# A weight quarter added by VectorE instead of an accumulating DMA, and weight buffers from a list instead of a ring

## The chip, the cores and the metric

One core of a Trainium2 chip runs the whole kernel as one program. The metric is the device time of one execution in microseconds, lower is better.

The core has five engines with queues of their own, each worked through in order: TensorE (PE: matmuls, and their weight loads, PEld), VectorE (DVE), ScalarE (ACT), GpSimd (POOL) and SyncE (SP). DMAs are issued from SP's queue or POOL's queue and run beside the engines. An engine that waits for a semaphore holds up all that stands behind in its queue.

## The reference

Two layers of a streaming encoder in float32, 512 tokens, width 1024. Cut to what matters:

```python
for i in range(2):
    h = h + 0.5 * swiglu_ffn(rms_norm(h, ffn1_norm[i]), ffn1_w_in[i], ffn1_w_out[i])
    u = rms_norm(h, mix_norm[i])
    ...                                    # SSD heads and latent attention on u @ w_in_mix[i]
    h = h + concat([y_ssd, y_mla]) @ w_out_mix[i]
    h = h + 0.5 * swiglu_ffn(rms_norm(h, ffn2_norm[i]), ffn2_w_in[i], ffn2_w_out[i])
    gate = sigmoid(rms_norm(h, ple_norm[i]) @ w_ple_gate[i])
    h = h + gate * (p[i] @ w_ple_proj[i])
return rms_norm(h, final_norm)

def swiglu_ffn(x, w_in, w_out):            # w_in: 1024 x 5632, w_out: 2816 x 1024
    g, u = jnp.split(x @ w_in, 2, axis=-1)
    return (jax.nn.silu(g) * u) @ w_out
```

So there are four FFN stages, two in each layer, and the change is in their first product, `x @ w_in`.

## The kernel before

**Precision.** Every float32 operand is split into two parts, `hi` (ScalarE's cast to the matmul's type, L300 for weights) and `lo` (VectorE's difference, L301). A product is three matmuls: hi by hi, hi by lo, lo by hi.

**The fast product.** In the FFN stages `x @ w_in` is computed for most columns in groups of 512, by a two-by-two scheme with seven block products in place of eight. There are nine groups in each stage (`NG`), 36 in all. For group `n` the weights are cut into four quarters of 512 x 256 by half of the inner dimension (`kh`) and half of the columns (`c`). Products 1, 2 and 3 (their numbers are names in the scheme) use the quarters (0,0), (1,0) and (1,1) as they are. Products 5, 6, 4 and 7 use sums of quarters, which are built in place, in a chain: 5 is 1's block plus quarter (0,1); 6 is 5's plus (1,1); 4 is 6's plus (1,0); 7 is 3's block plus (0,1). Each addition can start only when the block has been split for the product before it in the chain.

Before the groups come four whole blocks (`whole("g", f)`, f0 to f3), with which the norm's statistics overlap. The order of the products is written out: `FIRST_ORDER` for the first group (1, 5, 2, 3, 6) and `ORDER` for the others, where the 7 and the 4 of the group before are mixed in (1, 2, 7 of the group before, 5, 4 of the group before, 3, 6). The last group's 7 and 4 come after it, with whole blocks between them and behind.

**The units and their queue.** All weight blocks of the kernel stand in one list, `units`, in the order in which they are used. A unit either has a raw block of its own to load (`raws`, loaded by SP with L283, 512 KB in the FFN) or takes over the block of an earlier unit with something added. The function `weights(key)` hands out the next unit; before that it loads up to `LOOK_DMA` = 3 raw blocks beyond what the next units need and splits `LOOK_SPLIT` = 2 units ahead. `split_one` casts, subtracts and, where the block goes on in a chain (`more`), adds: by VectorE (L311) from another raw block, or by a DMA that accumulates from HBM into the block (L314, issued from POOL's queue).

In the kernel before, 5's and 7's additions are accumulating DMAs, 6's is a VectorE addition of 3's raw block before that is split, and 4's is a VectorE addition of 2's raw block, which was kept for it. A group has three loads, two accumulating DMAs and two VectorE additions.

**The raw buffers.** There are `NRAW` = 6 of 4 KB a partition, in one pool with one tag; a new tile takes a slot of this ring when the tile that held it is no longer used. The same ring gives temporaries: squares for the norms (L477 to L479), the FFN's output step (L762 to L765), and the attention's probabilities (L1260).

**Order on the engines.** The framework takes the program, and orders each engine's instructions by a simulated timeline; semaphores are set by it from the reads and writes of tiles.

Of the kernel before, what the change touches and what calls it, by code (L numbers as in the profile page):

```python
# [9 lines left out]
F32 = mybir.dt.float32  # L10
# [7 lines left out]
P = 128  # L18
# [77 lines left out]
def kernel(ctx: ExitStack, tc: tile.TileContext, a: dict, out: bass.AP):  # L96
# [5 lines left out]
    banks = _Slots(  # L102
        ctx.enter_context(tc.tile_pool(name="banks", bufs=1, space=bass.MemoryType.PSUM)), 8, "b"
    )
    p_raw = ctx.enter_context(tc.tile_pool(name="p_raw", bufs=NRAW))
    p_hi = ctx.enter_context(tc.tile_pool(name="p_hi", bufs=NW))
    p_lo = ctx.enter_context(tc.tile_pool(name="p_lo", bufs=NW))
    small = ctx.enter_context(tc.tile_pool(name="small", bufs=2))
# [6 lines left out]

    uid = [0]

    def tmp():

        uid[0] += 1  # L120
        return p_raw.tile([P, 1024], F32, tag="raw", name=f"tmp{uid[0]}")[:, :T]

    def sm(tag, shape, dt=F32, bufs=None):
        uid[0] += 1
# [12 lines left out]
    def raw(nk, cols, *loads):  # L137
        raws.append((nk, cols, loads))
        return len(raws) - 1
# [7 lines left out]
    def plan_ffn(i, nm, w_in, w_out):  # L147
        wq = w_in.rearrange("(k two p) f -> two p k f", two=2, p=P)

        def quarter(n, kh, c):  # L150
            x, q = GROUPS[n]
            c0 = q * 4 * P + (x == "u") * FF + c * 2 * P
            return [(slice(0, 2 * P), wq[kh, :, :, c0:c0 + 2 * P])]

        at = {}

        def quarter_unit(n, p):
            key = (i, nm, n, p)
            first = {1: (0, 0), 2: (1, 0), 3: (1, 1)}
            if p in first:  # L160
                unit(key, 4, 256, *quarter(n, *first[p]))
                at[n, p] = (len(units) - 1, units[-1][3])
            else:


                before = {5: 1, 6: 5, 4: 6, 7: 3}[p]
                add = {6: 3, 4: 2}.get(p)
                units.append((key, 4, 256, None, (at[n, before][0], quarter(n, 0, 1) if add is None else at[n, add][1])))
                at[n, p] = (len(units) - 1, None)

        def whole(x, f):
            unit((i, nm, x, f), KD, P, (None, kview(w_in, 0, KD, (x == "u") * FF + f * P, P)))

        for f in range(4):
            whole("g", f)
        for n in range(NG):
            for p, back in ORDER if n else FIRST_ORDER:
                quarter_unit(n - back, p)
        quarter_unit(NG - 1, 7)
        whole("g", LAST)  # L180
        quarter_unit(NG - 1, 4)
        whole("g", LAST + 1)
        whole("u", LAST)
        whole("u", LAST + 1)
        for m in range(KD):
            for k0 in range(0, KF, 8):
                nk = min(8, KF - k0)
                unit((i, nm, "o", m, k0), nk, P, (None, kview(w_out, k0, nk, m * P, P)))
# [70 lines left out]
    loaded, split, held = [], [], {}  # L259
    later = deque()  # L260
    more = {u[4][0]: j for j, u in enumerate(units) if u[4] is not None}

    def place_in(t, nk, cols, loads, start):
        v = t[:, :nk * cols].rearrange("p (k f) -> p k f", k=nk)
# [13 lines left out]
    def load_one():  # L278
        for _ in range(4 if len(loaded) > 2 else 0):
            if later:  # L280
                later.popleft()()
        t = p_raw.tile([P, 1024], F32, tag="raw", name=f"raw{len(loaded)}")
        place_in(t, *raws[len(loaded)], lambda dst, src: nc.sync.dma_start(out=dst, in_=src))  # L283
        loaded.append(t)

# [3 lines left out]
    def split_one():  # L289
        j = len(split)  # L290
        _, nk, cols, r, _ = units[j]
        if r is not None:
            while len(loaded) <= r:
                load_one()
            held[j] = loaded[r]
        x = held.pop(j)
        n = nk * cols
        hi = p_hi.tile([P, 1024], F32R, tag="hi", name=f"hi{j}")
        lo = p_lo.tile([P, 1024], F32R, tag="lo", name=f"lo{j}")
        A.copy(hi[:, :n], x[:, :n])  # L300
        V.tensor_tensor(lo[:, :n], x[:, :n], hi[:, :n].bitcast(F32), op=ALU.subtract)  # L301
        split.append((hi[:, :n].rearrange("p (k f) -> p k f", k=nk),
                      lo[:, :n].rearrange("p (k f) -> p k f", k=nk)))
        if j in more:

            held[more[j]] = x
            _, nk, cols, _, (_, add) = units[more[j]]
            if isinstance(add, int):
                while len(loaded) <= add:
                    load_one()  # L310
                V.tensor_tensor(x[:, :n], x[:, :n], loaded[add][:, :n], op=ALU.add)  # L311
            else:
                place_in(x, nk, cols, add,
                         lambda dst, src: G.dma_start(out=dst, in_=src, accum_op=ALU.add))  # L314

    taken = [0]

# [4 lines left out]
    def weights(key):  # L322
        j = taken[0]
        assert units[j][0] == key, (units[j][0], key)
        taken[0] += 1
        while len(loaded) < min(last_raw[min(j + LOOK_SPLIT, len(units) - 1)] + 1 + LOOK_DMA, len(raws)):
            load_one()
        while len(split) < min(j + 1 + LOOK_SPLIT, len(units)):
            split_one()
        got, split[j] = split[j], None  # L330
        return got
# [103 lines left out]
    class Norm:  # L435
# [36 lines left out]
        def add_square(self, src):  # L472
            if self.acc is None:
                self.acc = S()
                A.activation(self.acc.ap, src, AF.Square)
            else:
                sq = tmp()  # L477
                A.activation(sq, src, AF.Square)
                V.tensor_tensor(self.acc.ap, self.acc.ap, sq, op=ALU.add)  # L479

        @property
        def ops(self):
# [93 lines left out]
    def ffn(i, nm, norm, nxt, start=lambda: None, tables=lambda: None, between=lambda: None):  # L576
# [169 lines left out]
        for m in range(KD):  # L746
            b = B()
            for k0 in range(0, KF, 8):
                w = weights((i, nm, "o", m, k0))
                nk = w[0].shape[1]  # L750
                if m == 0:
                    while len(H) < min(k0 + nk, LAST):
                        split_pair(len(H) // 2)
                    if k0 + nk == KF:
                        split_last()
                acc_wx(b.ap, w, {f: (p.ap, q.ap) for f, (p, q) in H.items()}, k0, k0 == 0, k0 + 8 >= KF)
                if m == KD - 1:
                    for f in range(k0, k0 + nk):
                        slots.put(*H[f])
            if m == KD - 1:  # L760
                between()
            t = tmp()  # L762
            V.scalar_tensor_tensor(out=t, in0=b.ap, scalar=0.5, in1=norm.rb.ap, op0=ALU.mult, op1=ALU.mult)
            banks.put(b)
            V.tensor_tensor(h[m].ap, h[m].ap, t, op=ALU.add)  # L765
            nxt.add(h[m].ap)
        slots.put(norm.rb)

# [71 lines left out]
    def mixer(i, norm, nxt):  # L840
# [403 lines left out]
        def scores(hd, qb):  # L1244
            n = (qb + 1) * P
            qs = slice(qb * P, (qb + 1) * P)
            b = B()
            ql, kl = qh[hd], kh[hd]
            kr = st["kr"]
            mm(b[:, :n], lhsT=ql[0][:, qs], rhs=kl[0][:, :n], start=True, stop=False)  # L1250
            mm(b[:, :n], lhsT=ql[0][:, qs], rhs=kl[1][:, :n], start=False, stop=False)
            mm(b[:, :n], lhsT=ql[1][:, qs], rhs=kl[0][:, :n], start=False, stop=False)
            mm(b[:, :n], lhsT=qrow[hd][:, qs], rhs=kr[0][:, :n], start=False, stop=False)
            mm(b[:, :n], lhsT=qrow[hd][:, qs], rhs=kr[1][:, :n], start=False, stop=False)
            mm(b[:, n - P:n], lhsT=mk_l, rhs=mk_r, start=False, stop=True)
            m = sm("a_m", [P, 1], bufs=4)
            V.tensor_reduce(out=m, in_=b[:, :n], axis=AX.X, op=ALU.max)
            nb = sm("a_nb", [P, 1], bufs=4)
            V.tensor_tensor(nb, m, st["nsq"][:, qb:qb + 1], op=ALU.mult)
            pr = tmp()  # L1260
            rs = sm("a_rs", [P, 1], bufs=4)
            A.activation(pr[:, :n], b[:, :n], AF.Exp, bias=nb, scale=st["sq"][:, qb:qb + 1], accum_out=rs)
            banks.put(b)
            ri = sm("a_ri", [P, 1], bufs=4)
            V.reciprocal(ri, rs)
            V.tensor_scalar(pr[:, :n], pr[:, :n], ri, None, op0=ALU.mult)
            return pr
# [5 lines left out]
        def flip(hd, qb, pr, pt):  # L1273
            b = B()
            ks = order[qb]
            for n, kb in enumerate(ks):
                tr(b[:, n * P:(n + 1) * P], pr[:, kb * P:(kb + 1) * P], ident)  # L1277
            n = 0
            while n < len(ks):
                kb = ks[n]  # L1280
                w = 2 if (kb == 1 and qb == 3) else 1
                buf, c0 = place[kb]
                c0 += (qb - kb) * P
                src = b[:, n * P:(n + w) * P]
                halves(src, pt[0][buf][:, c0:c0 + w * P], pt[1][buf][:, c0:c0 + w * P])
                n += w
            banks.put(b)
# [284 lines left out]
```

## Time and profile before

| | |
|---|---|
| median of 3 runs | 2336.83 us (2334.89 to 2343.46) |
| the profiled execution's own time | 2346.55 us |
| its span, from the first to the last instruction | 2344.9 us |
| TensorE busy | 2295.8 us (98%) |
| VectorE busy | 1552.6 us (66%) |
| ScalarE busy | 1093.3 us (47%) |
| GpSimd busy | 215.5 us (9%) |
| moved by DMA | 229.01 MB, mean 98 GB/s |

How to read the profile: busy shares are means over stages. The groups of instructions give line, engine, operation, written and read tile, shape, count, then busy time, mean of one in ns, and the idle time of the engine just before them with what ended it (`<-`). In a timeline the first two numbers are start and duration in us, and a bracket gives the idle time before and its releaser. Rows of windows give the stretch, its length, then busy time and number of instructions for each engine, the granted TensorE clock as a share of full speed, the busy share of the 16 DMA engines, and GB/s. `raw` is a tile of the weight ring, `hi` and `lo` its two parts, `b` a PSUM bank, `s` a slot of working memory. L591 to L593 are the matmuls of the seven products, L418 to L420 those of whole blocks. The four FFN stages begin at about 0, 760, 1180 and 1920 us.

### The profile page before, as it was taken

Reading aid. Unit: us, or ns where it says so; the run is one execution under the profiler, and the core shown is the slowest. Engines: PE = TensorE matmul, PEld = TensorE weight load, DVE = VectorE, ACT = ScalarE, POOL = GpSimd, SP = SyncE. Lnnn points to the kernel's source line nnn. Section 1 sums busy time; section 2 is a strip of 40 time slices with the busy share of each in tenths; the row PEclk is TensorE's granted clock in tenths of the full one; section 3 lists DMA queues with packets and bytes.
Section 4 is the critical chain, followed back from the end, with each engine's and each line's share of the span. In section 5 each row is a group of like instructions: output and inputs, shape, how many; then the busy total and the mean of one; then the engine's idle time right before and its main releaser. Section 6 shows DMA issues by size and latency. Waiting matters only on the chain.

```text
span 2344.9 us, 34036 instructions
## 1 busy us (share of the span) xinstructions
PE 2295.8 (98%) x13542; PEld 2021.8 (86%) x13542; DVE 1552.6 (66%) x2456; ACT 1093.3 (47%) x1780; POOL 215.5 (9%) x208
## 2 busy tenths in 40 slices
PE   8999999999999899999999999999999999999998
PEld 6999888878888899888899988888788878998887
DVE  7878445678676777734777684466876776776345
ACT  6555324445455545522544452254544554454224
POOL 1110001132000111000011100012310001110000
PEclk9999999999999999999999999999999999999999
DMA  6555334311221465533345553342112225664332
GB/s 148 133 129 133 97 96 113 86 42 50 61 74 54 108 136 127 136 86 88 103 109 128 126 128 90 91 111 81 34 50 76 72 65 116 135 135 111 92 86 72
DMA packets 341420, 229.01 MB, mean 98 GB/s; under 512 B 20015, under 2 KB 335629, under 8 KB 341261
## 3 DMA queue, kind: packets, MB, share of 16 engines
q1 hardware_dynamic: 303244, 189.08, 27.5%
q0 software_dynamic: 38016, 37.75, 10.8%
q8 instruction: 106, 1.74, 0.3%
q14 instruction: 54, 0.43, 0.1%
HBM read 224.71 MB, written 2.10 MB: 97 GB/s over the span
## 4 chain that ended last, share of the span: by engine, by line
PE 81%; issue 10%; DVE 4%; DMA 2%; ACT 2%; POOL 1%; SPq 1%; POOLq 0%; ACTq 0%; DVEq 0%
PE b L418 15%; PE b L420 15%; PE b L419 15%; PE b L591 7%; PE b L593 7%; PE b L592 7%; DMA raw<-in_ffn_w_in_dram 2%; PE b L427 2%; PE b L426 2%; PE b L428 2%; DVE lo L301 1%; PE b L1112 1%; ACT hi L300 1%; PE b L1277 1%; DVE s L432 1%
## 5 line engine op out<-in xcount | busy, mean ns | idle before, releaser
L301 DVE TENSOR_TENSOR lo<-raw,hi 128x1024 fp32r<-128x1024 f32 (+3 forms) x536 | 612.4, 1143 | 469.6 <-ACT hi L300 469.0
L300 ACT CAST hi<-raw 128x1024 fp32r<-128x1024 f32 (+3 forms) x536 | 523.8, 979 | 855.6 <-PE b L419 411.5
L418 PE MATMUL b<-s,hi 128*128 128x512 f32 (+1 forms) x1754 | 693.5, 397 | 7.8 <-ACT hi L300 7.8
L420 PE MATMUL b<-s,lo 128*128 128x512 f32 (+1 forms) x1754 | 685.8, 392 | 6.5 <-DVE lo L301 6.5
L419 PE MATMUL b<-s,hi 128*128 128x512 f32 (+1 forms) x1754 | 683.8, 390 | 0.0
L591 PE MATMUL b<-s,hi 128*128 128x256 f32 x2016 | 574.4, 286 | 18.0 <-ACT hi L300 9.9
L592 PE MATMUL b<-s,hi 128*128 128x256 f32 x2016 | 572.0, 284 | 0.0
L593 PE MATMUL b<-s,lo 128*128 128x256 f32 x2016 | 567.9, 285 | 1.7 <-DVE lo L301 1.7
L591 PEld LDWEIGHTS b<-s,hi 128*128 128x128 f32 x2016 | 390.1, 193 | 23.5 <-ACT hi L300 11.7
L418 PEld LDWEIGHTS b<-s,hi 128*128 128x128 f32 x1754 | 330.6, 188 | 77.4 <-ACT hi L300 10.7
L420 PEld LDWEIGHTS b<-s,lo 128*128 128x128 f32 x1754 | 329.9, 188 | 77.6 <-DVE lo L301 8.8
L592 PEld LDWEIGHTS b<-s,hi 128*128 128x128 f32 x2016 | 390.2, 194 | 0.2
L593 PEld LDWEIGHTS b<-s,lo 128*128 128x128 f32 x2016 | 387.2, 193 | 2.6 <-DVE lo L301 2.5
L419 PEld LDWEIGHTS b<-s,hi 128*128 128x128 f32 x1754 | 330.5, 188 | 68.0 <-issue 2.9
L314 POOL DMA_DIRECT2D raw<-in_ffn_w_in_dram x72 | 92.8, 1289 | 850.5 <-DVE lo L301 819.2
L431 ACT CAST s<-b 128x128 fp32r<-128x128 f32 (+2 forms) x196 | 67.2, 361 | 99.8 <-DVE s L432 38.7
L431 ACT CAST s<-s 128x256 fp32r<-128x256 f32 (+1 forms) x248 | 94.2, 423 | 36.8 <-DVE s L611 13.2
L432 DVE TENSOR_TENSOR s<-s,s 128x256 fp32r<-128x256 f32 (+1 forms) x248 | 100.2, 442 | 9.8 <-PE b L593 7.4
L432 DVE TENSOR_TENSOR s<-b,s 128x128 fp32r<-128x128 f32 (+2 forms) x196 | 75.9, 401 | 30.2 <-ACT s L431 29.1
L503 POOL TENSOR_TENSOR nr<-nv,half 128x4 f32<-128x4 f32 (+1 forms) x14 | 20.2, 1439 | 813.1 <-DVE nv L495 812.3
L311 DVE TENSOR_TENSOR raw<-raw,raw 128x1024 f32<-128x1024 f32 x72 | 88.0, 1222 | 1.7
L426 PE MATMUL b<-hi,s 128*128 128x512 f32 (+1 forms) x208 | 78.5, 377 | 0.0
(245 smaller groups left out, 2247.7 us busy)
## 6 DMA issues: line engine op xcount, KB each, us to landing
raw<-in_ffn_w_in_dram SPq DMA_DIRECT2D x140, 512.0 KB
raw<-in_ffn_w_in_dram POOLq DMA_DIRECT2D x72, 512.0 KB, 5.9
raw<-in_ffn_w_out_dram SPq DMA_DIRECT2D x64, 512.0 KB
raw<-in_w_in_mix_dram SPq DMA_DIRECT2D x50, 512.0 KB
raw<-in_w_out_mix_dram SPq DMA_DIRECT2D x32, 512.0 KB
raw<-in_ffn_w_out_dram SPq DMA_DIRECT2D x32, 384.0 KB
raw<-in_w_ple_gate_dram SPq DMA_DIRECT2D x16, 512.0 KB
raw<-in_w_q_b_dram SPq DMA_DIRECT2D x16, 192.0 KB
```

The costliest lines, as they stand in the source:

```text
L300: A.copy(hi[:, :n], x[:, :n])
L301: V.tensor_tensor(lo[:, :n], x[:, :n], hi[:, :n].bitcast(F32), op=ALU.subtract)
L314: lambda dst, src: G.dma_start(out=dst, in_=src, accum_op=ALU.add))
L418: mm(b, lhsT=hi[:, kk, cs], rhs=xh, start=st, stop=False)
L419: mm(b, lhsT=hi[:, kk, cs], rhs=xl, start=False, stop=False)
L420: mm(b, lhsT=lo[:, kk, cs], rhs=xh, start=False, stop=en)
L426: mm(b, lhsT=xh[:, cs], rhs=hi[:, kk], start=first, stop=False)
L431: A.copy(hi, src)
L432: V.tensor_tensor(lo, src, hi.bitcast(F32), op=ALU.subtract)
L591: mm(o, lhsT=hi[:, k, cs], rhs=xh, start=first and f == k == 0, stop=False, **more)
L592: mm(o, lhsT=hi[:, k, cs], rhs=xl, start=False, stop=False, **more)
L593: mm(o, lhsT=lo[:, k, cs], rhs=xh, start=False, stop=f == 1 and k == 3, **more)
```

## The change

Quarter (0,1) gets a raw block of its own, loaded by SP right after product 1's block. Product 5's sum is a VectorE addition from it, behind the split of unit 1; the added block's buffer is then given back. Product 4's sum, until now a VectorE addition of 2's block, becomes an accumulating DMA of quarter (1,0) from HBM; 2's buffer is given back after its split. Products 6 and 7 are summed as before. A group has now four loads, two accumulating DMAs and two VectorE additions.

The six raw buffers have tags of their own and are given out from a list, the one that has been free longest first. They are given back in the program's text where the last use stands, for temporaries too. Loading ahead stops when only one buffer is free.

```diff
-    p_raw = ctx.enter_context(tc.tile_pool(name="p_raw", bufs=NRAW))
+    rawbufs = _Slots(ctx.enter_context(tc.tile_pool(name="p_raw", bufs=1)), NRAW, "raw")
...
-    def tmp():
-        uid[0] += 1
-        return p_raw.tile([P, 1024], F32, tag="raw", name=f"tmp{uid[0]}")[:, :T]
+    def W():
+        return rawbufs.get(F32, (P, 1024))
...
             if p in first:
                 unit(key, 4, 256, *quarter(n, *first[p]))
-                at[n, p] = (len(units) - 1, units[-1][3])
+                if p == 1:
+                    at[n, 0] = raw(4, 256, *quarter(n, 0, 1))
             else:
-                before = {5: 1, 6: 5, 4: 6, 7: 3}[p]
-                add = {6: 3, 4: 2}.get(p)
-                units.append((key, 4, 256, None, (at[n, before][0], quarter(n, 0, 1) if add is None else at[n, add][1])))
-                at[n, p] = (len(units) - 1, None)
+                before = at[n, {5: 1, 6: 5, 4: 6, 7: 3}[p]]
+                if p == 5:
+                    add = at[n, 0]
+                elif p == 6:
+                    add = units[at[n, 3]][3]
+                else:
+                    add = quarter(n, *{4: (1, 0), 7: (0, 1)}[p])
+                units.append((key, 4, 256, None, (before, add)))
+            at[n, p] = len(units) - 1
...
+    own = {u[3] for u in units}
...
-        t = p_raw.tile([P, 1024], F32, tag="raw", name=f"raw{len(loaded)}")
+        t = W()
         place_in(t, *raws[len(loaded)], lambda dst, src: nc.sync.dma_start(out=dst, in_=src))
...
-                V.tensor_tensor(x[:, :n], x[:, :n], loaded[add][:, :n], op=ALU.add)
+                y = loaded[add]
+                V.tensor_tensor(x[:, :n], x[:, :n], y[:, :n], op=ALU.add)
+                if add not in own:
+                    rawbufs.put(y)
             else:
                 place_in(x, nk, cols, add,
                          lambda dst, src: G.dma_start(out=dst, in_=src, accum_op=ALU.add))
+        else:
+            rawbufs.put(x)
...
-        while len(loaded) < min(last_raw[min(j + LOOK_SPLIT, len(units) - 1)] + 1 + LOOK_DMA, len(raws)):
+        while (len(loaded) < min(last_raw[min(j + LOOK_SPLIT, len(units) - 1)] + 1 + LOOK_DMA, len(raws))
+               and len(rawbufs.free) > 1):
             load_one()
```

The squares of the norms, the output step's temporary and the attention's probabilities take `W()` where they took `tmp()`, and each is followed by a `rawbufs.put` behind its last use.

More of the change, by code (lines that the diff above doesn't have):

```diff
@@ L476, in add_square @@
             else:
-                sq = tmp()
-                A.activation(sq, src, AF.Square)
-                V.tensor_tensor(self.acc.ap, self.acc.ap, sq, op=ALU.add)
+                sq = W()
+                A.activation(sq[:, :T], src, AF.Square)
+                V.tensor_tensor(self.acc.ap, self.acc.ap, sq[:, :T], op=ALU.add)
+                rawbufs.put(sq)
         @property
@@ L761, in ffn @@
                 between()
-            t = tmp()
-            V.scalar_tensor_tensor(out=t, in0=b.ap, scalar=0.5, in1=norm.rb.ap, op0=ALU.mult, op1=ALU.mult)
+            t = W()
+            V.scalar_tensor_tensor(out=t[:, :T], in0=b.ap, scalar=0.5, in1=norm.rb.ap, op0=ALU.mult, op1=ALU.mult)
             banks.put(b)
-            V.tensor_tensor(h[m].ap, h[m].ap, t, op=ALU.add)
+            V.tensor_tensor(h[m].ap, h[m].ap, t[:, :T], op=ALU.add)
+            rawbufs.put(t)
             nxt.add(h[m].ap)
@@ L1259, in scores @@
             V.tensor_tensor(nb, m, st["nsq"][:, qb:qb + 1], op=ALU.mult)
-            pr = tmp()
+            pr = W()
             rs = sm("a_rs", [P, 1], bufs=4)
@@ L1277, in flip @@
                 tr(b[:, n * P:(n + 1) * P], pr[:, kb * P:(kb + 1) * P], ident)
+            rawbufs.put(pr)
             n = 0
```

## The prediction

> **What bounds the kernel now.** I read the busy shares, the groups, the stage windows, the gaps of TensorE, and the queues of ScalarE and GpSimd around each gap.
>
> ```profile
> span 2344.9 us, 34036 instructions
> PE 2295.8 (98%) x13542; PEld 2021.8 (86%) x13542; DVE 1552.6 (66%) x2456; ACT 1093.3 (47%) x1780; POOL 215.5 (9%) x208
> ...
> L314 POOL DMA_DIRECT2D raw<-in_ffn_w_in_dram x72 | 92.8, 1289 | 850.5 <-DVE lo L301 819.2
> L311 DVE TENSOR_TENSOR raw<-raw,raw 128x1024 f32<-128x1024 f32 x72 | 88.0, 1222 | 1.7
> ```
>
> TensorE is the bound; no matmul is added or removed, so what can be won is its idle time (2344.9 - 2295.8 = 49 us) and time at a lowered clock. The windows show where that lies in the four FFN stages (columns: PE busy, weight loads, DVE, ACT, POOL, granted clock, DMA share, GB/s).
>
> ```profile
> core 0: us, PE busy (x) PEld busy (x) DVE busy (x) ACT busy (x) POOL busy (x), PEclk, DMA share, GB/s
> 40.00:60.00 20.00, 18.32 (x134) 17.73 (x133) 12.81 (x20) 10.66 (x14) 4.15 (x3) 0.91 0.58 130
> 780.00:800.00 20.00, 15.03 (x97) 14.11 (x96) 7.77 (x15) 6.75 (x9) 3.62 (x3) 0.83 0.45 88
> 800.00:820.00 20.00, 19.00 (x159) 18.82 (x158) 15.77 (x18) 11.17 (x15) 1.89 (x2) 1.00 0.49 114
> 820.00:960.00 140.00, 140.00 (x1169) 140.00 (x1168) 108.14 (x122) 72.11 (x96) 18.11 (x15) 1.00 0.60 132
> 1220.00:1340.00 120.00, 116.74 (x964) 115.69 (x964) 88.26 (x96) 58.30 (x74) 15.42 (x12) 1.00 0.57 126
> 1340.00:1360.00 20.00, 17.51 (x134) 17.34 (x133) 14.08 (x19) 8.41 (x13) 2.25 (x2) 0.91 0.49 113
> 1940.00:1960.00 20.00, 15.72 (x110) 15.22 (x109) 10.47 (x17) 10.15 (x14) 3.27 (x2) 0.83 0.37 61
> 1960.00:1980.00 20.00, 19.04 (x159) 18.87 (x158) 16.14 (x18) 8.83 (x11) 2.55 (x2) 1.00 0.55 122
> ```
>
> From 820 to 960 nothing is lost: a product of 24 matmuls takes 140 / 1169 x 24 = 2.87 us, a group of seven 20.1 us. The loss sits at the stage starts and along the third FFN stage. At the second stage's start:
>
> ```profile
> 779.02 1.33 POOL L314 DMA_DIRECT2D raw<-in_ffn_w_in_dram  x1 [110.95 <-DVE lo L301]
> ...
> 789.53 2.94 ACT L300 CAST hi<-raw 128x1024 fp32r<-128x1024 f32 x3 [11.50 <-DMA raw<-in_ffn_w_in_dram]
> ...
> 790.63 0.58 PE L591 MATMUL b<-s,hi 128*128 128x256 f32 x1 [4.50 <-ACT hi L300]
> ...
> 792.00:793.00 1.00, 1.00 (x5) 1.00 (x6) 1.00 (x2) 0.95 (x2) 1.00 (x1) 0.50 0.00 0
> ```
>
> In the first group product 5 comes right after product 1. Its weights are product 1's block with a quarter accumulated onto it by a DMA (L314), which starts only when unit 1 has been split. It needs 10.4 us; ScalarE, in order, stands 11.5 us at the cast of unit 5, with the casts of 2 and 3 behind it; TensorE stands 4.50 us, and the clock then falls to 0.50. The others are the same wait:
>
> ```profile
> 44.72 2.95 ACT L300 CAST hi<-raw 128x1024 fp32r<-128x1024 f32 x3 [6.40 <-DMA raw<-in_ffn_w_in_dram]
> ...
> 803.62 7.74 DMA raw<-in_ffn_w_in_dram
> 811.46 1.06 ACT hi L300
> ...
> 1218.20 1.05 ACT L300 CAST hi<-raw 128x1024 fp32r<-128x1024 f32 x1 [4.44 <-DMA raw<-in_ffn_w_in_dram]
> ...
> 1344.02 1.05 ACT L300 CAST hi<-raw 128x1024 fp32r<-128x1024 f32 x1 [4.65 <-DMA raw<-in_ffn_w_in_dram]
> ...
> 1945.67 2.94 ACT L300 CAST hi<-raw 128x1024 fp32r<-128x1024 f32 x3 [10.81 <-DMA raw<-in_ffn_w_in_dram]
> ...
> ACT hi L300 <- DMA raw<-in_ffn_w_in_dram: 82.8, 22, 11.5
> ```
>
> **The change part by part.**
>
> *Unit 5's sum goes from a DMA to VectorE.* The wait above goes away: behind the split of unit 1 stands one L311 add of 1.22 us instead of an accumulation of 7.7 to 10.4 us. The windows give what the waits cost. Idle: 1.68 + 4.97 + 1.00 + 3.26 + 2.49 + 4.28 + 0.96 = 18.6 us. Clock: 0.09 x 20 = 1.8 us in each of two windows; 0.17 x 20 = 3.4 us in each of the other two, of which some 0.8 falls on idle time counted already, so 2.6. Together 18.6 + 2 x 1.8 + 2 x 2.6 = 27.4 us. That is the most this part can give.
>
> The Trainium skill, "TensorE: Matmul & The Clock Gate", section "Why this matters for your kernels", has the clock drop only after TensorE gaps of some 3 us. By it the windows at 40 and 1340, with gaps of at most 1.68 and 2.49 us, would hold no clock loss and the gain would be 23.8 us. This trace disagrees (0.91 in both).
>
> What is late next at a stage start: the load of the added block. It stands in SP's queue directly behind unit 1's load, where unit 2's stood:
>
> ```profile
> 762.23 0.37 SPq L283 DMA_DIRECT2D raw<-in_ffn_w_in_dram  x1
> 769.03 0.37 SPq L283 DMA_DIRECT2D raw<-in_ffn_w_in_dram  x1
> 773.59 0.37 SPq L283 DMA_DIRECT2D raw<-in_ffn_w_in_dram  x1
> 776.18 3.88 SPq L283 DMA_DIRECT2D raw<-in_ffn_w_in_dram  x3
> ...
> 777.51 1.22 DVE L301 TENSOR_TENSOR lo<-raw,hi 128x1024 fp32r<-128x1024 f32 x1
> ```
>
> Counting the stage's loads (f0 to f3, 1, 2, 3), unit 1's is that of 762.23; the added block takes the place at 769.03, units 2 and 3 those of 773.59 and 776.18. Unit 1's split ends at 778.7, over 9 us after 769.03, so the add finds its data, unit 5 is cast by 781, and TensorE, which ran out at 786, has it in time. Units 2 and 3 come one load later but without the accumulation beside them. Residue 0, bounds 0 to 1 us a stage.
>
> *Unit 4's sum goes from VectorE to a DMA.* The adds stay 72 of 1.22 us: one moves from behind the split of 6 to behind that of 1, with three units between the adds as before; what is queued behind it on VectorE is the split of unit 2 and the combinations of products, which have a lookahead of two products (5.7 us). Zero; if that cover were gone, 36 x 1.22 = 44 us. The accumulations stay 72. Unit 4's starts after the split of 6 and is needed five units later (1, 2, 7, 5, 4), 14.3 us; unit 7's start and need stay as they are. On GpSimd nothing in a group waits behind them but each other. Their landing:
>
> ```profile
> DMA to landing us min/median/max: 5.6/5.9/10.4
> ...
> 213.50 1.28 POOL L314 DMA_DIRECT2D raw<-in_ffn_w_in_dram  x1 [13.05 <-DVE lo L301]
> ...
> 219.44 1.05 ACT L300 CAST hi<-raw 128x1024 fp32r<-128x1024 f32 x1 [1.11 <-DMA raw<-in_ffn_w_in_dram]
> ...
> 223.24 0.50 PE L418 MATMUL b<-s,hi 128*128 128x512 f32 x1 [0.85 <-ACT hi L300]
> ```
>
> Split (1.05 + 1.22) and even 10.4 us of landing fit into 14.3. Where it is tight is a stage's end: unit 7's cast already waits 1.11 us there, the next unit's cast is behind it and TensorE stands 0.85 us. Unit 4's accumulation now follows one product behind unit 7's and shares the engines with it. Bounds: 0 (the first lands in 5.9 us as now) to 10.4 - 5.9 = 4.5 us later, for each of four stages 0 to 18 us. I take 1 us each, near the lower end, since unit 7's starts first: 4 us.
>
> *36 loads of 512 KB more.* SP: 36 x 0.37 = 13 us of issue, hidden in its waiting; the DMA engines:
>
> ```profile
> q1 hardware_dynamic: 303244, 189.08, 27.5%
> ...
> SPq L283 <- DVE lo L301: 1226.5, 213, 22.2
> ```
>
> 0.275 x 2344.9 / 189.08 = 3.4 us per MB, so 1.8 us of 16 engines per load; in a group of 20.1 us the share goes from 0.60 to 0.69. Zero while the engines have room; 36 x 1.8 = 64 us if they had none.
>
> *A list instead of a ring.* I walked the list by hand for an FFN stage. In a group four buffers come free (the added block, unit 2's, 7's, 4's), each load takes the one freed an event before the last, so it can start six to seven units (17 to 20 us) before it is needed; in the ring unit 1's next block waits for unit 4's split, three units ahead (8.6 us). The free list never goes below one there. The squares and temporaries take the same list; at the first stage's start they rotate over three buffers. Bounds -2 to +3 us, taken 0.
>
> **Sum.** The profiled execution took 2346.55 us for its span of 2344.9 and is 9.7 us above the median. On its own time: 2346.55 - 27.4 + 4 = 2323.2. Against the median: if the third stage's chain of gaps (3.26 + 2.49 + 1.8 = 7.5 us), which the same code does not show in the other three stages, is most of the excess, 2336.83 - 19.9 + 4 = 2320.9; if none of it is, 2313.4. I take 2320, near the first, since that chain is nearly as long as the excess.
>
> **Rivals.**
> - *The wait moves to the stage ends.* The two accumulations, now one product apart among more loads, land late; the cast of unit 7 holds the next whole block up. For it: the 0.85 us gap there, and 10.4 us of landing while SP's loads ran. Against: unit 7's is issued first. Price: 4.5 us and 1.8 us of clock in each of two stages, 12.6: 2333; in all four, 2345. The Trainium skill, "DMA: Bandwidth & Descriptors", section "SWDGE vs HWDGE vs iDMA", has each DMA engine take turns between GpSimd's and SP's queues, which speaks for this. The 10.4 us beside three loads agrees with it.
> - *Slower: the add blocks VectorE.* In every group the add stands in order on the added block's load. If that comes later than 3.4 us (two products less 2.3 us of split) after unit 1's split, unit 2 is late and TensorE stands. At 4.5 us late, 1.1 us in 36 groups: 2320 + 40 = 2360. Against: 17 us of lead, and no cast waited for an SP load before.
> - *No gain.* TensorE meets another wait at the same places, such as unit 3's block for the add that makes unit 6: 2337. For it: VectorE runs 108 of 140 us there; against: the clean 140 us from 820.
>
> **How the numbers follow.** Forecast 0.62 (2311 to 2327), stage ends 0.22, blocking add 0.08, no gain 0.08. This measurement can tell some 0.5% (11.7 us) from nothing: faster means under 2325.1. Faster: the forecast less 0.04 above that bound, 0.58. Same: 0.04 + 0.18 of the stage ends + 0.08 = 0.30. Slower: 0.04 of the stage ends in full + 0.08 = 0.12. The range is 2310 to 2334, from the sum with no excess in the chain and the list's lower bound to the stage ends' first price; outside lie the blocking add, no gain and the tail of the stage ends.
>
> **What would show it.** Right: the casts' wait for DMA (82.8 us) falls under 20; the windows at the stage starts come to 20 us of TensorE at 1.00; L311 and L314 stay at 72; DMA bytes rise by 18.9 MB. Wrong: VectorE's add waiting on a load in many groups; TensorE gaps over 2 us at the stage ends; a chain of gaps that persists through a stage with unit 4's or 7's accumulation as its cause.

## The result, and the profile after

The changed kernel takes 2308.67 us (median of 5, 2306.83 to 2311.27) against 2336.83 us, 28.2 us less: ratio 0.9876, 95% interval 0.9857 to 0.9895. Forecast were 2320 us and a range that ended at 2310. The direction and the mechanism held; the gain was larger than forecast. The profiled execution took 2306.83 us, 39.7 us less than the one profiled before.

The page of the kernel after (L306 and L307 are now the weight split, L318 VectorE's addition, L323 the accumulating DMA, L604 the products' first matmul):

```profile
span 2305.1 us, 34208 instructions
PE 2278.3 (99%) x13542; PEld 2010.8 (87%) x13542; DVE 1563.9 (68%) x2456; ACT 1094.2 (47%) x1780; POOL 212.9 (9%) x208
...
DMA packets 360428, 247.89 MB, mean 108 GB/s; under 512 B 20590, under 2 KB 354636, under 8 KB 360268
...
L604 PE MATMUL b<-s,hi 128*128 128x256 f32 x2016 | 569.8, 283 | 1.6 <-ACT hi L306 1.6
L323 POOL DMA_DIRECT2D raw<-in_ffn_w_in_dram x72 | 92.7, 1287 | 586.2 <-DVE lo L307 567.7
L318 DVE TENSOR_TENSOR raw<-raw,raw 128x1024 f32<-128x1024 f32 x72 | 88.1, 1224 | 1.8
```

TensorE's idle time fell from 49.1 to 26.8 us (span less busy time), by 22.3 us. Its busy time fell by another 17.5 us although it runs the same 13542 matmuls: some of them were run at a lowered clock before, and the mean granted clock rose from 0.992 to 1.000. The additions and accumulations are 72 each as before, and the traffic rose by 18.9 MB. The products' first matmul before, with the idle time in front of it:

```profile
L591 PE MATMUL b<-s,hi 128*128 128x256 f32 x2016 | 574.4, 286 | 18.0 <-ACT hi L300 9.9 <-ACT s L608 6.4 <-DVE s L620 1.3
```

The products' 18.0 us went to 1.6. The windows of the kernel after, in the FFN stages:

```profile
core 0: us, PE busy (x) PEld busy (x) DVE busy (x) ACT busy (x) POOL busy (x), PEclk, DMA share, GB/s
40.00:60.00 20.00, 20.00 (x167) 19.77 (x167) 18.30 (x31) 14.29 (x20) 4.69 (x3) 1.00 0.79 194
200.00:220.00 20.00, 18.71 (x148) 17.93 (x148) 18.11 (x33) 15.10 (x31) 2.57 (x2) 1.00 0.64 137
760.00:780.00 20.00, 19.22 (x112) 16.39 (x111) 17.02 (x31) 9.16 (x14) 1.99 (x2) 1.00 0.42 132
780.00:940.00 160.00, 160.00 (x1336) 160.00 (x1335) 126.88 (x144) 84.38 (x112) 19.55 (x16) 1.00 0.68 156
940.00:960.00 20.00, 18.75 (x131) 17.19 (x130) 17.25 (x34) 14.95 (x34) 2.56 (x2) 1.00 0.67 146
1180.00:1340.00 160.00, 160.00 (x1335) 160.00 (x1335) 122.07 (x133) 80.66 (x105) 20.59 (x16) 1.00 0.69 158
1340.00:1360.00 20.00, 18.64 (x138) 17.39 (x137) 18.38 (x33) 14.24 (x30) 2.56 (x2) 1.00 0.62 134
1920.00:2080.00 160.00, 160.00 (x1335) 160.00 (x1334) 127.75 (x148) 85.51 (x114) 20.19 (x16) 1.00 0.67 157
2080.00:2100.00 20.00, 18.68 (x120) 16.66 (x119) 17.18 (x33) 13.66 (x30) 1.28 (x1) 1.00 0.68 148
```

Once a stage's products run, nothing is lost until the stage's end, the third stage included, and the clock is full in all these windows. The 0.78 us from 760 to 780 lie where the last whole block and the first product meet (0.53 us at the same place before). The DMA share in the groups is 0.68 where 0.69 was worked out. What is left in the stages are their ends, 1.29 + 1.25 + 1.36 + 1.32 = 5.2 us of idle time. The cast of unit 5, at which ScalarE had stood 11.5 us, in the timeline of ScalarE and VectorE after:

```profile
770.81 1.23 DVE L318 TENSOR_TENSOR raw<-raw,raw 128x1024 f32<-128x1024 f32 x1
...
772.14 1.05 ACT L306 CAST hi<-raw 128x1024 fp32r<-128x1024 f32 x1 [4.19 <-DVE raw L318]
773.51 1.05 ACT L306 CAST hi<-raw 128x1024 fp32r<-128x1024 f32 x1 [0.32 <-DMA raw<-in_ffn_w_in_dram]
```

Unit 5's cast follows the addition by a tenth of a microsecond, and unit 2's waits 0.32 us for its load.

### The profile page after: what moved, and what is told of

It is laid out like the page before. It is cut to its first block, busy times and chain, and to the rows that moved or that the text cites. A ratio compares the mean times of both kernels' runs of the same rounds, so it can differ in the third digit from the quotient of the medians.

```text
span 2305.1 us, 34208 instructions
## 1 busy us (share of the span) xinstructions
PE 2278.3 (99%) x13542; PEld 2010.8 (87%) x13542; DVE 1563.9 (68%) x2456; ACT 1094.2 (47%) x1780; POOL 212.9 (9%) x208
## 4 chain that ended last, share of the span: by engine, by line
PE 70%; issue 23%; DVE 3%; DMA 1%; ACT 1%; SPq 1%; POOL 1%; POOLq 0%; DVEq 0%; ACTq 0%
PE b L432 15%; PE b L430 15%; PE b L431 14%; PE b L606 5%; PE b L604 5%; PE b L605 5%; PE b L439 1%; PE b L438 1%; PE b L440 1%; DMA raw<-in_ffn_w_in_dram 1%; PE b L1126 1%; DVE lo L307 1%; PE b L1291 1%; PE b L1110 0%; PE b L502 0%
## 5 line engine op out<-in xcount | busy, mean ns | idle before, releaser
L306 ACT CAST hi<-raw 128x1024 fp32r<-128x1024 f32 (+3 forms) x536 | 524.2, 979 | 838.7 <-PE b L431 411.3
L307 DVE TENSOR_TENSOR lo<-raw,hi 128x1024 fp32r<-128x1024 f32 (+3 forms) x536 | 613.6, 1145 | 405.6 <-ACT hi L306 403.9
L604 PE MATMUL b<-s,hi 128*128 128x256 f32 x2016 | 569.8, 283 | 1.6 <-ACT hi L306 1.6
L604 PEld LDWEIGHTS b<-s,hi 128*128 128x128 f32 x2016 | 387.3, 192 | 3.4 <-ACT hi L306 2.9
L323 POOL DMA_DIRECT2D raw<-in_ffn_w_in_dram x72 | 92.7, 1287 | 586.2 <-DVE lo L307 567.7
L318 DVE TENSOR_TENSOR raw<-raw,raw 128x1024 f32<-128x1024 f32 x72 | 88.1, 1224 | 1.8
```

The lines of the kernel that those rows point to most:

```text
L604: mm(o, lhsT=hi[:, k, cs], rhs=xh, start=first and f == k == 0, stop=False, **more)
```

## The experiments

Two theories stood against each other at first: the gain is the removed wait on unit 5's accumulating DMA, with the clock that falls after TensorE's gaps (W); or the list's earlier loads give much of it (L). Then came the question of where in a stage the wait costs: mostly in the first groups (S), or in every group (C). Diffs are shortened; they are against the changed kernel, and for the first group's order against the kernel before. Each kernel has one profile, the changed one two. The kernel before took 2344.56 us beside the first four kernels and 2342.42 us beside the last four; each ratio is to the kernel before in the same comparison, and the expectations' times, written for 2336.83 us, are read by it.

**The list alone**

```diff
-                if p == 5: add = at[n, 0]          # and no raw block for quarter (0,1)
+                elif p == 4: add = units[at[n, 2]][3]
...
-                    add = quarter(n, *{4: (1, 0), 7: (0, 1)}[p])
+                    add = quarter(n, 0, 1)         # 5 and 7
...
-        else:
+        elif units[j][3] not in kept:              # 2's block stays for 4's sum
             rawbufs.put(x)
```

> The sums as in the kernel before (5 and 7 by accumulating DMA, 4 and 6 by VectorE, 2's block kept for 4), the buffers from the list. Theory W (the gain is the wait of unit 5's cast on its accumulating DMA, and the clock that falls after TensorE's gaps): as before, 2330 to 2345 us, ScalarE's casts wait 70 us or more for DMA, gaps of 4 to 5 us at the starts of the second and fourth FFN stage. Theory L (the list's earlier loads give much of the gain): 2325 us or less, with those gaps shorter.

Measured: 2344.83 us, ratio 0.9994 (0.9979 to 1.0008). The windows of this kernel:

```profile
780.00:800.00 20.00, 14.98 (x99) 14.32 (x98) 8.31 (x14) 6.69 (x9) 3.27 (x2) 0.83 0.48 86
820.00:960.00 140.00, 136.26 (x1114) 135.21 (x1113) 101.00 (x114) 67.34 (x88) 16.65 (x13) 0.99 0.60 128
1220.00:1300.00 80.00, 77.84 (x644) 77.15 (x643) 57.54 (x62) 37.86 (x46) 10.26 (x8) 1.00 0.58 127
1940.00:1960.00 20.00, 16.06 (x122) 15.65 (x122) 12.90 (x19) 11.54 (x15) 4.55 (x3) 0.91 0.41 85
```

The gap at the second stage's start is 5.02 us (4.97 before), the fourth's 3.94, and the chain of small gaps in the third stage is there. The second stage has one too in this profile, 3.74 us from 820 to 960. The casts wait 102.5 us for DMA. The list does nothing for the time by itself; theory L falls.

**Only 5's sum back to a DMA**

```diff
-                if p == 1: at[n, 0] = raw(4, 256, *quarter(n, 0, 1))
-                if p == 5: add = at[n, 0]
...
-                    add = quarter(n, *{4: (1, 0), 7: (0, 1)}[p])
+                    add = quarter(n, *{4: (1, 0), 5: (0, 1), 7: (0, 1)}[p])
```

> The changed kernel with 5's sum by an accumulating DMA again, so three accumulating DMAs and one VectorE addition in a group, list kept, no extra load. Theory W: the gaps are back, 2330 to 2350 us, casts wait 80 us or more for DMA. Theory L, or a gain that comes from taking 4's addition off VectorE: 2320 us or less.

Measured: 2344.01 us, ratio 0.9993 (0.9981 to 1.0006). The list is in, 4's addition is off VectorE, and the whole gain is gone; the casts wait 99.5 us for DMA, and the gaps at the starts of the second and fourth stage are 4.08 and 3.98 us. It is 5's sum that carries the gain.

**4's sum back to VectorE**

```diff
+                elif p == 4: add = units[at[n, 2]][3]
                 else:
-                    add = quarter(n, *{4: (1, 0), 7: (0, 1)}[p])
+                    add = quarter(n, 0, 1)
```

> The changed kernel with 4's sum by VectorE from 2's kept block, as before the change: three VectorE additions and one accumulating DMA in a group, four loads. Theory W: within 0.2% of the changed kernel, 2305 to 2313 us; the second gap at each stage's end (0.53 us after the change) is back near 0.97 us, 4 x 0.44 = 1.8 us in all. Rival V (4's move off VectorE carries a part): 2316 us or more.

Measured: 2316.49 us, ratio 0.9878 (0.9864 to 0.9893). On 2336.83 us that is 2308.3, the changed kernel's time (its ratio is 0.9876, and 0.9860 when it was run again): theory W. The time itself lies in V's bracket only because the kernel before took 2344.56 us in this comparison. Nor is it the number of accumulations that counts: the kernel before has two in a group and the last run three, both without the gain, and the changed kernel has two and this one has one, both with it. At the stage ends its windows lose more than the kernel after does:

```profile
200.00:220.00 20.00, 19.56 (x164) 19.36 (x162) 17.85 (x28) 13.40 (x27) 1.28 (x1) 1.00 0.48 114
220.00:240.00 20.00, 18.28 (x94) 15.27 (x95) 16.81 (x33) 11.40 (x25) 0.00 (x0) 0.91 0.41 121
940.00:960.00 20.00, 18.18 (x144) 17.40 (x143) 18.67 (x33) 15.03 (x32) 1.27 (x1) 1.00 0.54 131
960.00:980.00 20.00, 19.90 (x110) 17.12 (x109) 15.29 (x27) 9.66 (x20) 0.00 (x0) 1.00 0.47 136
1360.00:1380.00 20.00, 18.09 (x109) 15.49 (x108) 18.38 (x35) 13.63 (x31) 0.00 (x0) 1.00 0.48 139
2080.00:2100.00 20.00, 18.12 (x140) 17.18 (x139) 18.82 (x34) 14.59 (x31) 1.28 (x1) 1.00 0.52 124
```

Idle: 0.44 + 1.72 + 1.82 + 0.10 + 1.91 + 1.88 = 7.9 us against 5.2. As expected, the second gap of each end, which waits for VectorE's difference, is 0.98 us here at all four ends, where the kernel after has 0.53. So 4's move took 2.7 us of idle time out of the ends; in the times that is too little to tell.

**One product more for the accumulation**

```diff
-FIRST_ORDER = ((1, 0), (5, 0), (2, 0), (3, 0), (6, 0))
+FIRST_ORDER = ((1, 0), (2, 0), (5, 0), (3, 0), (6, 0))
```

> The kernel before with only the first group's order changed from 1, 5, 2, 3, 6 to 1, 2, 5, 3, 6, so unit 5's accumulating DMA has one more product (2.87 us) to land. Theory W: the gaps at the starts of the first, second and fourth FFN stage shrink by up to 2.87 us each (from 1.68, 4.97, 4.28) and the clock falls less: 2322 to 2332 us; the chain of small gaps in the third stage stays. If the order of products is not what the gaps hang on: 2333 to 2343 us.

Measured: 2334.84 us, ratio 0.9965 (0.9952 to 0.9977); on 2336.83 us that is 2328.7, inside theory W's bracket. The chain in the third stage is gone:

```profile
1200.00:1360.00 160.00, 160.00 (x1335) 160.00 (x1334) 121.61 (x135) 80.69 (x103) 20.55 (x16) 1.00 0.60 129
```

The gap at the second stage's start only fell to 4.37 us and the fourth's is 4.28, because at both a new wait took the old one's place. In the timelines:

```profile
792.25 1.11 PE L513 MATMUL b<-ident,nr 128*128 128x128 f32 x4 [4.37 <-POOL nr L503]
...
1937.80 1.99 ACT L300 CAST hi<-raw 128x1024 fp32r<-128x1024 f32 x2 [10.75 <-DMA raw<-in_ffn_w_in_dram]
1938.88 1.22 DVE L301 TENSOR_TENSOR lo<-raw,hi 128x1024 fp32r<-128x1024 f32 x1 [8.68 <-ACT hi L300]
1940.02 0.15 DVE L495 TENSOR_SCALAR nv<-b 128x4 f32<-128x4 f32 x1
1940.27 1.98 POOL L503 TENSOR_TENSOR nr<-nv,half 128x4 f32<-128x4 f32 x1 [11.19 <-DVE nv L495]
1942.31 1.12 PE L513 MATMUL b<-ident,nr 128*128 128x128 f32 x4 [4.28 <-POOL nr L503]
```

TensorE waits for the norm's spread (L513), which GpSimd's power (L503) released. Its input (L495) stands on VectorE behind the difference (L301) of unit 5, whose cast still waits 10.75 us for its DMA (up to 10.9 in this kernel). So the same DMA holds TensorE up by another way; that is read from the order of these lines, and no run parts the two. One part of the expectation fell: in this profile the third stage's chain does not stay.

**The changed kernel on one chip with three others**

> The changed kernel once more, beside the three below on one chip. Both theories: 0.986 to 0.990 of the time before. If what sets the spread of the kernel before is the clock that falls after TensorE's gaps, this one's granted clock is 0.997 or more in every run and its times lie within 6 us of each other; if the spread comes from DMA, they spread as before, some 15 us.

Measured: 2311.30 us, ratio 0.9860 (0.9839 to 0.9881). Granted clocks of its runs are 0.997 to 0.999 with times of 2307.95 to 2313.40; the kernel before beside it has 0.992 to 0.994 and 2338.59 to 2351.92. Both signs that theory W gave for the spread came, in four runs. They do not show that the clock is the whole of it: the nine runs of the kernel before spread over 13.3 us, and 0.002 of 2342 us is only 4.7.

**The wait back in the first groups only, and in all the others only**

```diff
-                if p == 1:
+                if p == 1 and n > 0:        # e5: first groups by DMA; e6: n == 0, the other groups by DMA
                     at[n, 0] = raw(4, 256, *quarter(n, 0, 1))
...
-                if p == 5:
+                if p == 5 and n > 0:        # e6: n == 0
                     add = at[n, 0]
...
-                    add = quarter(n, *{4: (1, 0), 7: (0, 1)}[p])
+                    add = quarter(n, *{4: (1, 0), 5: (0, 1), 7: (0, 1)}[p])
```

> The changed kernel, but in the first group of each FFN stage 5's sum is by an accumulating DMA again (no added block there); the other 32 groups as changed. Theory S (most of the gain is at the stage starts): it gives back 1.68 + 4.97 + 4.28 = 10.9 us of idle time and some 7 us of clock, so 14 to 20 us over the changed kernel; no gaps later in the stages. Theory C (the wait in every group matters as much): at most 8 us over the changed kernel.

> The changed kernel, but in all groups but the first of each stage 5's sum is by an accumulating DMA again. Theory S: 0 to 8 us over the changed kernel, no gap at the stage starts; small gaps in later groups only if they are a standing contention (then some 3 to 8 us), none if they were an echo of the late start. Theory C: 10 us or more over.

Measured: first groups by DMA 2328.58 us, 17.3 us over the changed kernel, ratio 0.9933 (0.9915 to 0.9952); the others by DMA 2323.74 us, 12.4 us over, ratio 0.9918 (0.9899 to 0.9938). The two add up to 29.7 of the 31.1 us on this chip. Windows with only the first groups by DMA:

```profile
780.00:800.00 20.00, 15.39 (x106) 14.89 (x106) 10.24 (x17) 8.61 (x11) 4.55 (x3) 0.83 0.58 115
800.00:960.00 160.00, 160.00 (x1336) 160.00 (x1335) 126.25 (x144) 84.21 (x115) 20.49 (x16) 1.00 0.68 156
1180.00:1340.00 160.00, 160.00 (x1290) 157.85 (x1289) 118.83 (x134) 79.96 (x102) 21.20 (x16) 1.00 0.65 149
```

The starts' gaps are back (4.61 us in the second stage), and nothing follows them inside the stages shown. Waits and windows with all other groups by DMA:

```profile
ACT hi L306 <- DMA raw<-in_ffn_w_in_dram: 61.5, 28, 3.0
...
220.00:240.00 20.00, 17.61 (x87) 14.60 (x86) 16.43 (x32) 13.02 (x28) 0.00 (x0) 0.91 0.50 136
780.00:920.00 140.00, 140.00 (x1170) 140.00 (x1169) 99.16 (x113) 72.46 (x92) 27.97 (x22) 1.00 0.77 159
940.00:960.00 20.00, 17.50 (x137) 16.61 (x136) 17.14 (x30) 14.97 (x31) 2.56 (x2) 0.96 0.69 144
1200.00:1340.00 140.00, 140.00 (x1167) 139.90 (x1167) 100.16 (x111) 70.49 (x91) 26.10 (x21) 1.00 0.75 155
1360.00:1380.00 20.00, 17.55 (x101) 15.09 (x101) 16.82 (x34) 13.09 (x28) 0.00 (x0) 1.00 0.63 150
```

ScalarE waits 28 times, 61.5 us, and inside the stages TensorE loses only 0.7 us (one gap of 0.31 in the first stage and one of 0.37 in the fourth). So in these profiles neither a late first group nor a DMA in each later group alone makes a chain of gaps as in the third stage before. The two together can make one, but not in each stage, and what decides which stage gets it no run shows. The cost of this kernel is at the stage ends, with about 2.5 us of gaps at each against 1.3 in the changed kernel, and a lowered clock. Theory S named the place of the larger part and missed the smaller: its 0 to 8 us had no price for the ends, and 12.4 us lies where theory C had put it.

**A version that beats both: the last group's order**

```diff
+LAST_ORDER = ((1, 0), (2, 0), (5, 0), (3, 0), (7, 1), (4, 1), (6, 0))
...
-            for p, back in ORDER if n else FIRST_ORDER:
+            for p, back in order_of(n):     # LAST_ORDER for n == NG - 1, in the plan and in the products
```

> The changed kernel with the last group's order 1, 2, 5, 3, then 7 and 4 of the group before, then 6, so that unit 7's accumulating DMA starts two products earlier. If the gap at the stage ends (1.25 to 1.36 us each, 5.2 us in all) hangs on that DMA: 2 to 5 us under the changed kernel, ratio 0.985 to 0.987. If it hangs on ScalarE's other work there: no change within 1 us.

Measured: 2303.56 us, 7.7 us under the changed kernel on the same chip, ratio to the kernel before 0.9828 (0.9809 to 0.9848). More than expected. The stage ends in its windows:

```profile
200.00:220.00 20.00, 20.00 (x167) 19.74 (x165) 19.03 (x32) 15.77 (x32) 2.57 (x2) 1.00 0.76 161
780.00:960.00 180.00, 180.00 (x1476) 178.63 (x1475) 144.65 (x180) 101.16 (x145) 22.95 (x18) 1.00 0.69 155
1180.00:1380.00 200.00, 200.00 (x1586) 196.19 (x1586) 154.78 (x190) 105.24 (x153) 23.16 (x18) 1.00 0.67 153
1920.00:2100.00 180.00, 180.00 (x1457) 177.81 (x1456) 144.40 (x178) 99.85 (x146) 20.47 (x16) 1.00 0.69 158
```

All four ends are without a gap. Of the 7.2 us between the profiled executions of the two kernels on this chip, 5.1 are idle time of TensorE (28.6 to 23.5 us) and 2.1 its busy time at 13542 matmuls in both (2280.4 to 2278.3), so the clock.

## Why the prediction was right in kind and wrong in size

*Unit 5's sum.* Right, place and price. The wait at the starts, the 800 and 1960 windows and the third stage's chain are gone, with their 18.6 us of idle time; the casts' wait for accumulating DMAs fell from 82.8 us to 4.1. Its 27.4 us is nearly the whole change of the median, and the run with 4's sum back on VectorE, in which of the sums only 5's has moved, took 2344.56 - 2316.49 = 28.1 us off.

*The added block's load.* Right: it is there when VectorE adds, and the blocking add did not come.

*The median's excess.* This step failed. It took 7.5 us off the gain, because the third stage's chain was held to be what lifted the profiled execution above the median. The list-only kernel, with the same sums, has such a chain in two stages, in an execution below that kernel's median (2341.53 of 2344.83). So a chain there does not make an execution a slow one, and the whole 27.4 us should have been taken. Nor is it true that the same code shows no chain in other stages. That the median execution of the kernel before itself has the chain is inferred, since only one execution of it was profiled.

Where the excess of 9.7 us came from instead is only in part known. A part of what varies between executions is the clock: in 28 runs on one chip the two of the kernel before at a granted clock of 0.990 took 2352.47 and 2353.26 us, the two at 0.995 took 2337.78 and 2341.00. One thousandth is 2.3 us, so the clock's range is worth 11.7 us of a spread of 15.7; runs at the same 0.993 still differ, from 2339.47 to 2346.92. The profile before has 0.992, and windows at a lowered clock outside the sum's four. The next lines show these and the stage ends, in the kernel before:

```profile
20.00:40.00 20.00, 17.25 (x68) 13.39 (x67) 15.30 (x37) 12.63 (x29) 1.47 (x1) 0.91 0.33 90
220.00:240.00 20.00, 18.06 (x102) 15.35 (x102) 16.38 (x32) 13.31 (x30) 0.00 (x0) 0.91 0.41 121
500.00:520.00 20.00, 18.87 (x92) 15.60 (x92) 12.24 (x16) 9.07 (x14) 5.61 (x5) 0.91 0.15 39
960.00:980.00 20.00, 18.20 (x125) 16.27 (x124) 17.46 (x36) 13.60 (x31) 0.49 (x1) 1.00 0.51 126
1380.00:1400.00 20.00, 18.05 (x109) 15.52 (x109) 17.98 (x34) 14.03 (x31) 0.00 (x0) 1.00 0.48 140
2120.00:2140.00 20.00, 18.04 (x112) 15.79 (x112) 15.97 (x32) 13.07 (x29) 0.00 (x0) 0.91 0.40 109
```

Four of them (20, 220, 500, 2120) hold 4 x 1.8 = 7.2 us, near the excess of 9.7. That the median execution had the full clock there is not shown: its clock was not recorded. And the excess itself hangs on the comparison: the same kernel's median was 2336.83 us here and 2344.56 and 2342.42 in the two later ones, 2.0 and 4.1 us below the profiled execution.

*The stage ends.* The second step that failed: plus 4 us, with a gain left out of the bounds without a reason. The four ends (220, 960, 1380, 2120) lost 1.94 + 1.80 + 1.95 + 1.96 = 7.7 us before and lose 5.2 after. Unit 7's accumulation was not delayed by 4's: at the four ends its cast waited 0.97 to 1.13 us for it before and 0.97 to 1.08 after. And VectorE no longer has 4's addition to do there: the second gap fell from 0.97 or 0.98 to 0.53 us at each end, and came back to 0.98 in the run that gave 4's sum back to VectorE. That the ends are tight was right, as the last order shows.

*The sum again.* On the profiled executions: 27.4 + 2.5 at the ends + 7.2 of clock elsewhere = 37.1 of the 39.7 us; the rest is 1.2 us of idle time at the kernel's start and the stage changes (22.3 - 18.6 - 2.5) and 1.4 unassigned. Against the median, without the discount and with the ends' sign right: 2336.83 - 27.4 - 2.5 = 2306.9, where 2308.67 was measured. This puts terms of a profiled execution against a median, so that it comes so near is partly luck.

*List, loads, SP, VectorE.* Right at zero in the measured sum, the list by its own run. The rival at the stage ends did not come; with three accumulations in a group it does (the run with all other groups by DMA).

## What to carry to other kernels

Of a chain of in-place sums, give the first link, whose product follows soonest, to the engine that is in order and near, and the link with the most products ahead of it to the slow DMA. Price a gap of the bound engine with the clock that it costs, and compare the granted clock of the profiled execution with the others before blaming a difference between runs on a wait. A wait in every group may cost next to nothing where there is cover, and the same wait costs at the two places where the cover is missing, here a stage's first group (17.3 us) and its end (12.4 us).

## What the runs showed of the hardware

Gaps far shorter than the one at 790 us went with a lowered clock, and not in each execution: the window at 500 us before (1.13 us idle) has 0.91, and so has this one of the changed kernel run again (1.15 us), where the first profile after shows 1.00 with 1.14 us:

```profile
480.00:500.00 20.00, 18.85 (x92) 15.19 (x91) 15.99 (x21) 7.94 (x11) 7.55 (x6) 0.91 0.24 59
```

```profile
480.00:500.00 20.00, 18.86 (x103) 15.58 (x102) 14.79 (x20) 7.48 (x11) 7.54 (x7) 1.00 0.28 73
```

The Trainium skill, "TensorE: Matmul & The Clock Gate", section "What's actually happening", sets the clock by how busy the array was in a window of about 3.4 us. The single gap of 1.1 us in these windows is shorter than that, and the clock fell behind it in two of the three; which condition decides, no run here shows.
